# A macaron block with an RWKV mixer: weight sums of the second gate/up phase made in DRAM beforehand, and six seven-product steps a block instead of four

## The chip, the core and the metric

The kernel runs on one core of one Trainium2 chip. The metric is the device time of one execution in microseconds (us), the median of several runs. Before the change it is 1986.32 us (three runs, 1985.78 to 1986.51).

## What is computed

One layer for 256 tokens of width 2048, all in float32: a half-weighted SwiGLU feed-forward (FFN), a mixer (an RWKV-7 scan branch and a pooling branch), and a second FFN.

```python
D_MODEL = 2048; SEQ = 256; D_FF = 5632
def _swiglu(x, w_gate, w_up, w_down):
    return (jax.nn.silu(x @ w_gate) * (x @ w_up)) @ w_down
...
f = _swiglu(_rmsnorm(h, ln_ffn1_pre[l]), ffn1_gate[l], ffn1_up[l], ffn1_down[l])
h = h + MACARON_WEIGHT * _rmsnorm(f, ln_ffn1_post[l])
mx = _hybrid_mixer(_rmsnorm(h, ln_mix_pre[l]), w_in[l], ...)
h = h + _rmsnorm(mx, ln_mix_post[l])
f = _swiglu(_rmsnorm(h, ln_ffn2_pre[l]), ffn2_gate[l], ffn2_up[l], ffn2_down[l])
h = h + MACARON_WEIGHT * _rmsnorm(f, ln_ffn2_post[l])
```

Each gate and up matrix is 2048 x 5632, each down matrix 5632 x 2048. All weights are streamed from DRAM while the products run.

## The kernel before, in words

**Products in three parts.** A float32 operand is split into a high part, rounded by ScalarE (`CAST` to `wH`), and a low part, `wL = w - wH`, by VectorE (`split`). A product is three matmuls (`mm3`): high by high, high by low, low by high. So each weight tile of 128 x 1024 costs ScalarE one cast, VectorE one subtraction, and TensorE twelve matmuls of 512 columns (two row tiles, two halves of the tokens, three parts). The instructions are recorded and emitted later, so every one of them stands at line 525 in the profile, and work is told apart by the names of the tiles.

**The gate/up phase.** The 5632 columns are eleven blocks of 512. A block multiplies the tokens by 512 columns of gate (`f`) and of up (`l`), for two token halves. Its 16 row tiles go in pairs k, k+1. A pair is done either plainly (`Columns.pair`: 24 matmuls for the pair, from two loads of 512 KB) or as a "quad" in Winograd's form of Strassen's method: seven products instead of eight, 21 matmuls. With w(k,l), w(k,f), w(k+1,l), w(k+1,f) for the four weight tiles of 128 x 512 (row tile k or k+1, up or gate), the weight side needs two first sums, kept in `t13`: w(k,l) + w(k,f) and w(k+1,f) + w(k,f); then `t2` = w(k,l) + the second of them; and the last sum `t4` = w(k+1,l) + t2. `Columns.early` loads the tiles, makes the sums and does four of the products; `Columns.late` loads w(k+1,f) and w(k+1,l) once more into `vc` and does the other three, t4 among them. Between them stands `join`, which adds the four part results in PSUM. The table `GATE2` (L50, `GATE1` at L49 for the first FFN) gives the quads of each block: none in the first two, three in the third, then four. `block_seq` (L1016) interleaves a block's own pairs and its late quads with the early quads of the block after it.

Of four quads in a block one (index 3, `GATE_ACC`, L56) has its t13 made by transfers: two loads of w(k,f), then two accumulating transfers issued by GpSimd (`accum_op`). The other three have t13 made by VectorE in one `t<-w,w` instruction of 128 x 1024. The same is done with two of the ten quads in each half of the down phase (`DOWN_ACC`, L55, in `Columns.quad`).

**Who sets the order.** `Plan` simulates the five engines, the transfers and the buffers, and emits each engine's instructions in the order that it finds. TensorE's products stand in the order of the code; VectorE, ScalarE, GpSimd (POOL) and SyncE (SP, which issues nearly all loads) take the ready instruction with the earliest due time. On the chip each engine then executes its list strictly in order, and waits on semaphores where its inputs are not there. Loads go into five buffers `w32` and borrowed "units" (`u`), split weights into five `wH` and `wL`.

**Stages by time in the profile:** first gate/up to about 452 us, first down phase to 687, mixer (input projections `w_in`, two scan chains of small steps, output projections) to about 1340, second gate/up to 1740, second down to the end. In the mixer the chain's small steps run among large products: its `Z` tiles are copied and its powers `g`, `n`, `rs` computed on POOL.

**`KEPT`** (L116): the gate/up results are turned and pass through DRAM (`cx`); of the first `KEPT` tiles of four the split halves are made at once and the raw copy is fetched again for the quads of the down phase, of the later ones the raw copy stays in SBUF and is split when the down phase comes to it. The down phase's quads begin at row tile 4 * `KEPT`. `normed` makes the normalised tokens, and `sums` the token-side sums that the quads need, one call for two quads.

## Time and profile before

| what | value |
|---|---|
| median of three runs | 1986.32 us |
| the profiled execution's own time | 1987.15 us |
| its span, first to last instruction | 1985.4 us |
| TensorE busy | 1974.6 us (99%), 9692 matmuls |
| VectorE busy | 1813.0 us (91%) |
| ScalarE busy | 1210.7 us (61%) |
| GpSimd busy | 118.8 us (6%) |
| moved by the 16 DMA engines | 503.19 MB, 253 GB/s on the mean |
| granted TensorE clock | 0.999 |

The span is 1.75 us shorter than the profiled execution's time, which is 0.83 us above the median. Busy rows of one engine may overlap by the pipeline's depth: where VectorE's instructions follow each other without a gap, the distance between two starts is the price, not the row's length. A row of a chain "x12" is twelve instructions after each other. In rows by windows, (x) is the number of instructions, DMA the busy share of the 16 DMA engines, and GB/s what they moved.

### The profile page before, as it was taken

What the parts mean: (1) busy time and instruction counts of PE and PEld (TensorE: products, weight loads), DVE (VectorE), ACT (ScalarE), POOL (GpSimd) and SP (SyncE); (2) the same over time, 40 slices, a digit from 0 to 9 for tenths busy, and PEclk for the clock granted to TensorE, in tenths of its full rate; (3) what the DMA queues carried; (4) which work ended last, traced back from release to release, by engine and by line L of the source; (5) the groups of instructions that cost most, each with busy time, mean ns of one, the idle gap of its engine ahead of it and who ended that gap; (6) DMA issues with size and microseconds to landing.
All of it is one profiled execution on the core that took longest, in us unless ns stands there. A gap on an engine that the chain in (4) does not pass through costs nothing.

```text
span 1985.4 us, 28410 instructions
## 1 busy us (share of the span) xinstructions
PE 1974.6 (99%) x9692; PEld 1630.8 (82%) x9692; DVE 1813.0 (91%) x2303; ACT 1210.7 (61%) x1552; POOL 118.8 (6%) x190
## 2 busy tenths in 40 slices
...
GB/s 319 323 266 283 276 317 312 278 257 228 242 198 274 261 259 277 216 167 252 178 194 190 128 322 262 240 258 241 273 307 293 317 287 286 255 230 236 204 287 144
DMA packets 278000, 503.19 MB, mean 253 GB/s; under 512 B 25056, under 2 KB 53472, under 8 KB 277856
## 3 DMA queue, kind: packets, MB, share of 16 engines
q1 hardware_dynamic: 267280, 478.96, 73.6%
q0 software_dynamic: 10144, 22.03, 5.3%
...
## 4 chain that ended last, share of the span: by engine, by line
PE 94%; DVE 3%; DMA 1%; ACT 1%; issue 1%; SPq 0%; POOLq 0%; ACTq 0%; DVEq 0%
PE l L525 33%; PE f L525 30%; PE mm L525 22%; PE p L525 6%; DVE wL L525 1%; DMA w<-in_ffn_gate_dram 1%; PE pY L525 0%; PE pA L525 0%; ACT wH L525 0%; PE tr L525 0%; PE pU L525 0%; DMA w<-in_ffn_down_dram 0%; DVE AR L525 0%; DMA w<-in_w_in_dram 0%; PE pSa L525 0%
## 5 line engine op out<-in xcount | busy, mean ns | idle before, releaser
L525 ACT CAST wH<-w 128x1024 fp32r<-128x1024 f32 (+1 forms) x712 | 727.4, 1042 | 508.4 <-PE f L525 105.1
L525 DVE TENSOR_TENSOR wL<-w,wH 128x1024 fp32r<-128x1024 f32 (+1 forms) x712 | 848.8, 1209 | 92.8 <-ACT wH L525 68.8
L525 PE MATMUL l<-wL,xH 128*128 128x512 f32 x828 | 322.3, 389 | 0.0
L525 PE MATMUL l<-wH,xL 128*128 128x512 f32 x828 | 322.2, 389 | 0.0
L525 PE MATMUL l<-wH,xH 128*128 128x512 f32 x828 | 322.1, 389 | 0.0
L525 PE MATMUL f<-wH,xH 128*128 128x512 f32 x608 | 236.6, 389 | 0.0
L525 PE MATMUL f<-wH,xL 128*128 128x512 f32 x608 | 236.6, 389 | 0.0
L525 PE MATMUL f<-wL,xH 128*128 128x512 f32 x608 | 236.5, 389 | 0.0
L525 PE MATMUL mm<-wL,xH 128*128 128x512 f32 (+1 forms) x568 | 220.2, 388 | 1.1 <-DVE wL L525 1.1
L525 PE MATMUL mm<-wH,xH 128*128 128x512 f32 (+1 forms) x568 | 220.8, 389 | 0.5 <-ACT xH L525 0.5
L525 PE MATMUL mm<-wH,xL 128*128 128x512 f32 (+1 forms) x568 | 219.1, 386 | 0.0
L525 ACT CAST wH<-t 128x1024 fp32r<-128x1024 f32 (+1 forms) x158 | 165.3, 1046 | 81.6 <-PE f L525 32.3
L525 DVE TENSOR_TENSOR wL<-t,wH 128x1024 fp32r<-128x1024 f32 (+1 forms) x158 | 191.5, 1212 | 17.0 <-ACT wH L525 7.9
L525 PEld LDWEIGHTS l<-wL,xH 128*128 128x128 f32 x828 | 155.4, 188 | 32.4 <-DVE wL L525 0.2
L525 PEld LDWEIGHTS l<-wH,xH 128*128 128x128 f32 x828 | 155.4, 188 | 32.3
L525 PEld LDWEIGHTS l<-wH,xL 128*128 128x128 f32 x828 | 155.4, 188 | 32.2
L525 DVE TENSOR_TENSOR t<-w,w 128x1024 f32<-128x1024 f32 (+1 forms) x170 | 167.2, 988 | 7.5 <-DMA w<-in_ffn_down_dram 5.6
L525 PEld LDWEIGHTS f<-wL,xH 128*128 128x128 f32 x608 | 114.1, 188 | 23.7
L525 PEld LDWEIGHTS f<-wH,xL 128*128 128x128 f32 x608 | 114.1, 188 | 23.7
L525 PEld LDWEIGHTS f<-wH,xH 128*128 128x128 f32 x608 | 114.1, 188 | 23.6
L525 PEld LDWEIGHTS mm<-wL,xH 128*128 128x128 f32 x568 | 106.8, 188 | 22.7 <-DVE wL L525 2.3
L525 PEld LDWEIGHTS mm<-wH,xH 128*128 128x128 f32 x568 | 106.7, 188 | 22.5 <-ACT xH L525 0.9
...
## 6 DMA issues: line engine op xcount, KB each, us to landing
w<-in_w_in_dram SPq DMA_DIRECT2D x120, 512.0 KB, 4.5
w<-in_ffn_up_dram SPq DMA_DIRECT2D x106, 512.0 KB, 5.1
w<-in_ffn_up_dram SPq DMA_DIRECT2D x210, 256.0 KB, 5.1
w<-in_ffn_gate_dram SPq DMA_DIRECT2D x102, 512.0 KB, 6.0
w<-in_ffn_gate_dram SPq DMA_DIRECT2D x202, 256.0 KB, 5.0
w<-in_ffn_down_dram SPq DMA_DIRECT2D x96, 512.0 KB, 4.8
w<-in_ffn_down_dram SPq DMA_DIRECT2D x152, 256.0 KB, 4.1
cx<-T SPq DMA_DIRECT2D x33, 512.0 KB, 3.8
```

The source lines that it names most:

```text
L525: ins = o.fn(*[real(x) for x in o.a], **{n: real(x) for n, x in o.k.items()})
```

## The change

1. `GATE2` becomes 0, 0, 6, 6, 6, 6, 6, 6, 6, 6, 5: 53 quads in place of 35 in the second gate/up phase. `GATE1` is as before.
2. `prepare` and `feed`: the two first sums of these 53 quads are made in DRAM ahead of time, for two blocks together. A job copies 128 x 1024 of gate from DRAM to a DRAM tile `pre` (issued by SP), and then adds 128 x 1024 of up or gate to it by an accumulating transfer (issued by POOL, which first waits for the copy). There are 58 jobs, 48 of 512 KB and ten of 256 KB (the last block is alone). They are handed to the planner little by little during the first down phase (0.4 for each pair) and the mixer (1.6 for each of its items), and a job's copy waits for the accumulation three jobs before it.
3. `GMODE2`: in the second gate/up phase `early` loads t13 from `pre` by two transfers on SP, which wait until VectorE has made t13's low part three quads before (`FLIGHT`). Quads of even index (mode 5): ScalarE copies t2 to t4, and one accumulating transfer adds w(k+1,l) from DRAM. Quads of odd index (mode 12): ScalarE copies t2 to t4, and in `late` VectorE adds w(k+1,l) from the tile `vc` that is loaded there anyway. In both, w(k,f), w(k+1,f) and the first w(k+1,l) are not loaded any more.
4. `GMODE1` is 8 for all quads of the first FFN: t13 by VectorE in all (none by transfers), t4 as in mode 12. `DOWN_ACC` goes: in the down phases t13 is made by VectorE in all quads (mode 0).
5. `KEPT` goes from 4 to 3. The planner's own numbers for an accumulating transfer change (`ADDING`, `ADD_RATE`), and it hands out jobs only while its list of transfers is short (`IDLE`).

POOL's list in the first scan chain of the mixer, before. `Z` are the chain's copies, `g` the powers of its group norm:

```order
L525 COPY Z_7508<-ev_7490 64x256
L525 COPY Z_7508<-od_7501 64x256
L525 TENSOR_TENSOR g_1795_9106<-g_1794_9093,mhalf 128x4
L525 COPY Z_7508<-ev_7490 64x256
L525 COPY Z_7508<-od_7501 64x256
L525 TENSOR_TENSOR g_1805_9194<-g_1804_9185,mhalf 128x4
L525 TENSOR_TENSOR g_1815_9323<-g_1814_9307,mhalf 128x4
```

The same place after; `pre` are the accumulations of the jobs:

```order
L540 COPY Z_7586<-ev_7571 64x256
L540 COPY Z_7586<-od_7575 64x256
L540 DMA pre_4_1_119<-in_ffn_gate_dram 128x1024
L540 TENSOR_TENSOR g_1795_9191<-g_1794_9176,mhalf 128x4
L540 DMA pre_5_0_120<-in_ffn_up_dram 128x1024
L540 COPY Z_7586<-ev_7571 64x256
L540 COPY Z_7586<-od_7575 64x256
L540 TENSOR_TENSOR g_1805_9286<-g_1804_9271,mhalf 128x4
L540 DMA pre_5_1_121<-in_ffn_gate_dram 128x1024
L540 TENSOR_TENSOR g_1815_9374<-g_1814_9360,mhalf 128x4
```

Three accumulations now stand between the chain's own steps on POOL; the steps' order among themselves is the same.

SP's list at the same place of the mixer, before (`w` are weights on their way to the products, `cx` and `x` the chain's passage through DRAM):

```order
L525 DMA w_1967_8854<-in_w_in_dram 128x2x512
L525 DMA w_1970_8893<-in_w_in_dram 128x2x512
L525 DMA w_1973_8965<-in_w_in_dram 128x2x512
L525 DMA w_2114_9039<-in_w_in_dram 128x2x512
L525 DMA cx_110<-T_1946_9063 128x2x512
```

And after:

```order
L540 DMA w_1967_8960<-in_w_in_dram 128x2x512
L540 DMA w_1970_9013<-in_w_in_dram 128x2x512
L540 DMA pre_4_1_119<-in_ffn_gate_dram 128x1024
L540 DMA pre_5_0_120<-in_ffn_gate_dram 128x1024
L540 DMA pre_5_1_121<-in_ffn_gate_dram 128x1024
L540 DMA w_1973_9098<-in_w_in_dram 128x2x512
L540 DMA w_2114_9141<-in_w_in_dram 128x2x512
L540 DMA cx_168<-T_1946_9169 128x2x512
```

Three copies of 512 KB now stand ahead of the next weights.

VectorE's list in the middle of the second gate/up phase, before: the sum t13 of two tiles (128x1024), t2 (`w<-w,t`), t4, and low parts `wL`:

```order
L525 TENSOR_TENSOR t_3012_14486<-w_3013_14392,w_3014_14400 128x1024
L525 TENSOR_TENSOR w_3013_14392<-w_3013_14392,t_3012_14486 128x512
L525 TENSOR_TENSOR t_2992_14417<-w_3014_14400,w_3013_14392 128x512
L525 TENSOR_TENSOR wL_14503<-t_2989_14390,wH_14444 128x1024
L525 TENSOR_TENSOR wL_14513<-w_3001_14351,wH_14464 128x1024
L525 TENSOR_TENSOR wL_14523<-w_3004_14360,wH_14482 128x1024
```

And after, in the same block:

```order
L540 TENSOR_TENSOR w_2973_14306<-w_2973_14306,t_2974_14382 128x512
L540 TENSOR_TENSOR wL_14520<-t_2875_14015,wH_14490 128x1024
L540 TENSOR_TENSOR w_2982_14330<-w_2982_14330,t_2983_14450 128x512
L540 TENSOR_TENSOR wL_14537<-w_2973_14306,wH_14522 128x1024
L540 TENSOR_TENSOR wL_14546<-t_2974_14382,wH_14529 128x1024
L540 TENSOR_TENSOR wL_14559<-w_2979_14319,wH_14540 128x1024
L540 TENSOR_TENSOR wL_14573<-w_2982_14330,wH_14548 128x1024
L540 TENSOR_TENSOR wL_14584<-t_2983_14450,wH_14556 128x1024
L540 TENSOR_TENSOR t_2899_14217<-t_2899_14217,w_2989_14348 128x512
```

The 128x1024 sum is gone; more low parts stand between the quads' own sums, and the last row is a t4 finished from the late tile (mode 12).

The diff, cut to its core:

```diff
 GATE1 = [0, 0, 3, 4, 4, 4, 4, 4, 4, 4, 4]
-GATE2 = [0, 0, 3, 4, 4, 4, 4, 4, 4, 4, 4]
+GATE2 = [0, 0, 6, 6, 6, 6, 6, 6, 6, 6, 5]
 OUT_QUADS = ((3, 4, 1.0), (3, 1, 1.0))
 DOWN1 = ((10, 1, 2.0), (10, 1, 1.3))
 DOWN2 = ((10, 1, 2.0), (10, 1, 1.3))
 SCRATCH = 1024
-DOWN_ACC = 6, 8
-GATE_ACC = 3,
+PRE = 2
+FLIGHT = 3
+BACK = 3
+OWN = 2
+IDLE = 2200.0
+PRE_DOWN = 0.4
+PRE_MIX = 1.6
+ADD_RATE = 190.0
+GMODE1 = [[8] * 8] * 11
+GMODE2 = [[5, 12, 5, 12, 5, 12]] * 11
+DMODE1 = [0] * 18, [0] * 18
+DMODE2 = DMODE1
...
-ADDING = 3000.0
+ADDING = 800.0
...
-KEPT = 4
+KEPT = 3
...
+            if "accum_op" in k:
+                o.pace = 1000.0
+                o.dur = o.nbytes / ADD_RATE
...
         def can(o):
+            if o.stream == "back" and dma > now + IDLE:
+                return False
...
-    def four(s, k):
-        q = s.b
-        t13 = q.unit((P, 2, 512), F32, "t13")
-        if k not in s.dma:
-            va, vb = q.raw4(k, s.wf, s.cf, s.wl, s.cl)
-            q.nc.vector.tensor_tensor(out=t13, in0=va,
-                                      in1=vb[:, :1].to_broadcast([P, 2, 512]), op=ALU.add)
-            return va, vb, t13
-        get = lambda k, f: (s.wf if f else s.wl)[k * P:k * P + P,
-                                                 (s.cf if f else s.cl):][:, :512]
-        for i in range(2):
-            q.nc.sync.dma_start(out=t13[:, i], in_=get(k, 1))
-        va, vb = [q.raw().rearrange("p (a c) -> p a c", a=2) for _ in range(2)]
-        q.nc.sync.dma_start(out=va[:, 0], in_=get(k, 0))
-        q.nc.sync.dma_start(out=va[:, 1], in_=get(k + 1, 1))
-        q.nc.sync.dma_start(out=vb[:, 1], in_=get(k + 1, 0))
-        for i in range(2):
-            q.nc.gpsimd.dma_start(out=t13[:, i], in_=get(k + i, i), accum_op=ALU.add)
-        return va, vb, t13
+    def at_w(s, k, f):
+        w, c = (s.wf, s.cf) if f else (s.wl, s.cl)
+        return w[k * P:k * P + P, c:c + 512]
+
+    def load(s, out, k, f):
+        s.b.nc.sync.dma_start(out=out, in_=s.at_w(k, f))
+
+    def plus_w(s, out, k, f):
+        s.b.nc.gpsimd.dma_start(out=out, in_=s.at_w(k, f), accum_op=ALU.add)
 
     def early(s, k):
         q = s.b
         V = q.nc.vector
-        va, vb, t13 = s.four(k)
-        V.tensor_tensor(out=va[:, 1], in0=va[:, 0], in1=t13[:, 1], op=ALU.add)
+        add = lambda o, x, y: V.tensor_tensor(out=o, in0=x, in1=y, op=ALU.add)
         i = s.quads.index(k)
+        mode = s.mode(i)
+        va = q.raw(mode & OWN).rearrange("p (a c) -> p a c", a=2)
+        s.load(va[:, 0], k, 0)
+        if mode & 4:
+            t13 = q.unit((P, 2, 512), F32, "t13")
+            with q.set(behind=q.done[-FLIGHT] if len(q.done) >= FLIGHT else None):
+                for j in range(2):
+                    q.nc.sync.dma_start(out=t13[:, j], in_=s.ready(i, j))
+        else:
+            vb = q.raw(mode & OWN).rearrange("p (a c) -> p a c", a=2)
+            s.load(vb[:, 0], k, 1)
+            s.load(va[:, 1], k + 1, 1)
         if i % 2 == 0:
             s.t4[i] = q.unit((P, 2, 512), F32, "t4")
-        V.tensor_tensor(out=s.t4[i - i % 2][:, i % 2], in0=vb[:, 1], in1=va[:, 1],
-                        op=ALU.add)
-        b11, t2 = q.halves(va)
-        t1, t3 = q.halves(t13)
+        t4 = s.t4[i - i % 2][:, i % 2]
+        if mode & 2:
+            s.plus_w(vb[:, 0], k, 0)
+            s.plus_w(va[:, 1], k, 1)
+            t2 = vb[:, 1]
+            add(t2, va[:, 0], va[:, 1])
+        else:
+            if not mode & 4:
+                if not mode & 9:
+                    s.load(vb[:, 1], k + 1, 0)
+                t13 = q.unit((P, 2, 512), F32, "t13")
+                add(t13, va, vb[:, :1].to_broadcast([P, 2, 512]))
+            t2 = va[:, 1]
+            add(t2, va[:, 0], t13[:, 1])
+        if mode & 9:
+            q.nc.scalar.copy(t4, t2)
+            if mode & 1:
+                s.plus_w(t4, k + 1, 0)
+        else:
+            if mode & 2:
+                s.load(t4, k + 1, 0)
+                add(t4, t4, t2)
+            else:
+                add(t4, vb[:, 1], t2)
+        if mode & 2:
+            b11, t3 = q.halves(va)
+            t1, t2 = q.halves(vb)
+        else:
+            b11, t2 = q.halves(va)
+            t1, t3 = q.halves(t13)
+            q.done.append(q.last_low)
...
         b22, b21 = q.halves(vc)
         i = s.quads.index(k)
-        if i % 2 == 0:
-            s.h4 = q.halves(s.t4[i][:, :min(2, len(s.quads) - i)])
         s.mul("f0", s.sm[k // 2][3], b22)
         s.mul("l0", s.rows(k + 1, 0), b21)
-        s.mul("l1", s.rows(k + 1, 1), s.h4[i % 2])
+        t4 = s.t4[i - i % 2][:, i % 2]
+        if s.mode(i) & 8:
+            q.nc.vector.tensor_tensor(out=t4, in0=t4, in1=vc[:, 1], op=ALU.add)
+        if i % 2 or k == s.quads[-1]:
+            i -= i % 2
+            two = s.quads[i:i + 2]
+            for k, w in zip(two, q.halves(s.t4[i][:, :len(two)])):
+                s.mul("l1", s.rows(k + 1, 1), w)
...
+    def prepare(s, wg, wu, quads, modes):
+
+        s.made = {}
+        nc = s.nc
+        nb = len(quads)
+        blocks = [b for b in range(nb) if any(m & 4 for m in modes[b][:quads[b]])]
+        for g in range(0, len(blocks), PRE):
+            bs = blocks[g:g + PRE]
+            c0, w = bs[0] * 512, len(bs) * 512
+            for i in range(max(quads[b] for b in bs)):
+                if not any(modes[b][i] & 4 for b in bs if i < quads[b]):
+                    continue
+                k = 2 * i
+                for j, (m, kk) in enumerate(((wu, k), (wg, k + 1))):
+                    d = s.dram((P, w), f"pre{g}_{i}_{j}")
+                    for n, b in enumerate(bs):
+                        s.made[b, i, j] = d[:, n * 512:n * 512 + 512]
+
+                    def job(d=d, m=m, k=k, kk=kk, c0=c0, w=w):
+                        with s.set(stream="back", behind=s.last[-BACK], lag=0.0):
+                            nc.sync.dma_start(out=d, in_=wg[k * P:k * P + P, c0:c0 + w])
+                            s.last.append(nc.gpsimd.dma_start(
+                                out=d, in_=m[kk * P:kk * P + P, c0:c0 + w], accum_op=ALU.add))
+                    s.jobs.append(job)
+
+    def feed(s, n):
+        s.owed += n
+        while s.owed >= 1 and s.jobs:
+            s.owed -= 1
+            s.jobs.pop(0)()
...
-            jobs[b].dma = [2 * i for i in GATE_ACC if i < quads[b]]
+            jobs[b].mode = lambda i, b=b: modes[b][i]
+            jobs[b].ready = lambda i, j, b=b: s.made[b, i, j]
...
-               downs, 4 * KEPT, DOWN_ACC)
+               downs, 4 * KEPT, downm)
...
+            J.mode = lambda i, c=c: acc[c // 2][i] if acc else 0
...
+                s.feed(PRE_DOWN)
                 J.pair(k, b)
...
+            s.feed(PRE_MIX)
...
+        s.feed(1e9)
...
+        s.prepare(ffn2_gate[0], ffn2_up[0], GATE2, GMODE2)
...
-              GATE1, DOWN1, (load, turn, squares, finish, scaled))
+              GATE1, DOWN1, GMODE1, DMODE1, (load, turn, squares, finish, scaled))
...
-              at_tok(h2), emit, load_to(h2, lambda h: hsp[1, h]), GATE2, DOWN2)
+              at_tok(h2), emit, load_to(h2, lambda h: hsp[1, h]), GATE2, DOWN2, GMODE2, DMODE2)
```

36 lines of the change are left out of this document (28 added, 8 removed).

## The prediction

> **What bounds the kernel now.** I read the page's busy times first, then who TensorE waited for, then the chain that ended last, then busy times by stage.
>
> ```profile
> span 1985.4 us, 28410 instructions
> PE 1974.6 (99%) x9692; PEld 1630.8 (82%) x9692; DVE 1813.0 (91%) x2303; ACT 1210.7 (61%) x1552; POOL 118.8 (6%) x190
> PE mm L525 <- DVE wL L525: 1.9, 4, 0.7
> PE warm L525 <- POOL ident masks.py:199: 1.5, 1, 1.5
> PE 94%; DVE 3%; DMA 1%; ACT 1%; issue 1%; SPq 0%; POOLq 0%; ACTq 0%; DVEq 0%
> ```
>
> TensorE is idle for 10.8 of 1985.4 us, its longest list of waits is 1.9 us, and 94% of the chain is its own work. Where is even that idle time? The first and the last window of the stages:
>
> ```profile
> 0.00:51.00 51.00, 48.44 (x212) 39.47 (x213) 40.01 (x55) 45.08 (x71) 3.48 (x9) 1.00 0.91 321
> 1945.80:1985.40 39.60, 33.29 (x143) 26.25 (x141) 22.40 (x34) 11.06 (x18) 1.10 (x2) 0.96 0.37 124
> ```
>
> 2.6 us at the start and 6.3 us at the end (second number against the first, the window's length); 1.9 us are left for everything between. So the kernel is as long as its list of matmuls, at a price that the chain in order of time gives:
>
> ```profile
> 1460.30 2.72 PE f L525 x12
> 1465.06 11.56 PE l L525 x51
> ```
>
> 11.56 / 51 = 0.2267 us for one 512-column matmul, with the granted clock at 1.00 in the stage rows. The question is what taking matmuls out leaves as the next limit. In four blocks in the middle of the second gate/up phase (columns: PE, PEld, DVE, ACT, POOL, clock, DMA share, GB/s):
>
> ```profile
> 1505.80:1546.60 40.80, 40.80 (x182) 33.78 (x181) 39.05 (x41) 23.67 (x27) 1.70 (x2) 1.00 0.88 282
> 1546.60:1587.40 40.80, 40.80 (x182) 33.78 (x181) 38.03 (x40) 24.38 (x27) 1.73 (x2) 1.00 0.97 317
> 1587.40:1628.20 40.80, 40.80 (x182) 33.78 (x181) 37.40 (x40) 24.80 (x27) 1.73 (x2) 1.00 0.90 285
> 1628.20:1669.00 40.80, 40.80 (x182) 33.78 (x181) 38.87 (x42) 25.22 (x27) 1.76 (x2) 1.00 0.92 296
> ```
>
> A block lasts 40.80 us = 180 matmuls, and VectorE is busy for 37.4 to 39.1 of it: idle 9.85 us in the four, 2.5 a block. It is the next engine in line.
>
> **TensorE: what goes.** 53 quads for 35 is 18 more, three matmuls saved in each: 54 x 0.2267 = 12.24 us. They lie on the path, since TensorE has no idle time there. Nothing else changes TensorE's list. A six-quad block has 174 matmuls and lasts 39.44 us if TensorE alone sets it.
>
> **VectorE in these blocks.** Starts give the prices, as nothing stands between them:
>
> ```profile
> 1466.07 1.22 DVE L525 TENSOR_TENSOR wL<-w,wH 128x1024 fp32r<-128x1024 f32 x1
> 1467.20 1.22 DVE L525 TENSOR_TENSOR t<-w,w 128x1024 f32<-128x1024 f32 x1
> 1468.34 0.69 DVE L525 TENSOR_TENSOR l<-l,s 128x512 f32<-128x512 f32 x1
> 1468.94 0.69 DVE L525 TENSOR_TENSOR f<-f,s 128x512 f32<-128x512 f32 x1
> ```
>
> 1.135 us for 1024 columns, 0.60 for 512. Before, a block has 22 low parts (8 of plain pairs, 3.5 in each quad), 3 sums t13, 4 t2, 4 t4, and 6 other sums of 512 and a transposition of 1024 for joining and evacuating: 26 x 1.135 + 14 x 0.60 = 37.9 us, which the busy times above bear out. After: 4 + 6 x 3.5 = 25 low parts, no t13, 6 t2, 3 t4, the same 6 and 1: 26 x 1.135 + 15 x 0.60 = 38.5 us. So VectorE's list grows by 0.6 us a block while the block shrinks by 1.36: its slack falls from 2.9 to 0.9 us. Most of its 2.5 us idle now is there because it is ahead of TensorE, and such idle time gives way when it falls behind. What does not give way is the time in which it waits for something of its own. The waits of VectorE from 1424 to 1740.5 us:
>
> ```profile
> DVE wL L525 <- issue: 4.5, 4, 2.6
> DVE wL L525 <- PE f L525: 4.4, 7, 1.2
> DVE wL L525 <- ACT wH L525: 4.1, 4, 2.2
> DVE wL L525 <- PE l L525: 2.4, 5, 1.5
> ```
>
> PE rows are waiting for a buffer: VectorE is ahead. ScalarE's 4.1 us over about eight blocks is 0.5 a block, with "issue" 1.1. Set against a slack of 0.9, that is a loss of 0 to 0.2 us a block. Bounds for eight blocks: nothing (all idle time gives way), and, if the 2.5 us of today stay whole, 38.5 + 2.5 - 39.44 = 1.5 each, 12 us. I take 1.5 us, near the lower end, because the waits that are VectorE's own are near the slack.
>
> Edits beside it, with these rows:
>
> ```profile
> L525 ACT CAST wH<-w 128x1024 fp32r<-128x1024 f32 x16 | 16.3, 1054 | 11.2 <-PE f L525 4.2 <-PE l L525 4.0 <-DMA w<-in_ffn_up_dram 3.0
> L525 ACT COPY u<-l 128x512 f32<-128x512 f32 x2 | 1.2, 584 | 0.0
> L525 DVE TENSOR_TENSOR sf<-x 128x256 f32<-128x256 f32 x24 | 9.1, 421 | 0.0
> L525 POOL DMA_DIRECT2D t<-in_ffn_gate_dram x16 | 14.1, 879 | 678.8 <-DMA t<-in_ffn_gate_dram 152.7 <-PE l L525 140.0 <-DMA w<-in_ffn_gate_dram 111.9
> ```
>
> ScalarE gets one 512-column copy for each quad (t2 to t4) and three more casts a block; it is busy for 23.7 to 25.2 of 40.8 us above, and its cast costs 1.05 us, its copy 0.6: 3 x 1.05 + 6 x 0.6 = 6.8 us more, 32 of 39.4. Hidden. The new third call of `sums` adds four 256-column sums and a low part, 4 x 0.42 + 1.14 = 2.8 us of VectorE in block 1, once. The first gate/up phase has one more t13 on VectorE in the eight four-quad blocks: 37.9 + 1.1 = 39.0 of 40.8 us, and it loses the accumulating transfers there. The down phases put two t13 more in each half on VectorE, 4.5 us in a phase:
>
> ```profile
> 452.00:687.00 235.00, 234.47 (x1040) 193.77 (x1039) 218.42 (x250) 143.72 (x169) 12.49 (x37) 1.00 0.75 240
> ```
>
> 218.4 + 4.5 of 235 us leaves 12 us. Hidden behind TensorE's matmuls; without that cover it would be 1.1 us for each. `KEPT` moves one split per FFN from the gate/up phase to the down phase. I cost these at nothing.
>
> **Transfers.** In the second gate/up phase they hardly change: a block of six quads loads 4 x 512 KB for plain pairs, 33 x 256 KB for quads (three of them accumulations), 10.7 MB for 39.44 us, where it loaded 8 x 512 KB and 27 x 256 KB, 11.3 MB, for 40.80. New are the 58 jobs in the first down phase and the mixer. 48 x 0.524 + 10 x 0.262 = 27.8 MB copied and 27.8 MB accumulated, beside what runs there now; and what the 16 engines can move:
>
> ```profile
> 40.00:60.00 20.00, 20.00 (x90) 16.57 (x89) 20.00 (x25) 16.12 (x23) 0.00 (x0) 1.00 1.05 407
> 445.00:1130.00 685.00, 683.04 (x3988) 563.82 (x3987) 617.83 (x973) 421.09 (x617) 70.97 (x124) 1.00 0.71 219
> q1 hardware_dynamic: 267280, 478.96, 73.6%
> q0 software_dynamic: 10144, 22.03, 5.3%
> ```
>
> The loads named on SP beside the jobs stand in the trace of before from about 445 to 1130 us, so that is their stretch: 55.6 MB / 685 us = 81 GB/s on top of 219. If an accumulation costs two loads, because it reads two operands, 41 more: 341 GB/s against 407 that plain loads reach at their best. That fits with a sixth to spare, and so I cost the contention at nothing on the mean. For what it does locally (TensorE loses 685 - 683.04 = 2.0 us in that stretch today, at the turn to the mixer and in the chain), from -1.9 (all idle time between start and end gone) to a copy's own time, 0.524 / 0.407 = 1.3 us, at each of perhaps three places where loads are already late. I take 0.5 us.
>
> **Waits on queues.** A job's copy stands on SP and waits for the accumulation three jobs back; behind it stand the weights of the mixer's products and the chain's `x` and `cx`. The accumulation stands on POOL and waits for its copy; behind it stand `Z`, `g`, `n`, `rs` of the chain, for which VectorE and TensorE wait. Jobs are 685 / 58 = 12 us apart, three jobs 36; and a landing takes
>
> ```profile
> w<-in_w_in_dram SPq DMA_DIRECT2D x120, 512.0 KB, 4.5
> t<-in_ffn_up_dram POOLq DMA_DIRECT2D x16, 256.0 KB, 6.8
> ```
>
> 4.5 us for a load of a copy's size, 6.8 for an accumulation of half a job's. Copy and accumulation together are under 20 us even if the accumulation doubles, so SP should not stand still. The two loads of t13 wait on SP for VectorE's work three quads back, some 20 us: nothing, while VectorE keeps up.
>
> **Sum.** 12.24 - 1.5 - 0.5 = 10.2 us off the span: 1985.4 - 10.2 = 1975.2. The profiled execution is 1987.15 us, 1.75 over its span, and 0.83 above the median of 1986.32; so 1976.1 for the median.
>
> **Rivals.**
> *VectorE becomes the bound of the second gate/up phase.* For: a list of 38.5 in 39.44 us. Against: its idle time today is mostly room. Price 5 to 12 us of the 12.24, with SP's t13 loads held up as well: 1979 to 1986. Decides from 0.9 us of its own waits a block.
>
> *The jobs fill the DMA engines; slower.* Place: 445 to 1130 us. If data passing through DRAM costs once for each reading and writing (copy 2, accumulation 3), the jobs are 139 MB, 203 GB/s: 422 against 407, and the stretch grows by 685 x (422/407 - 1) = 25 us. By the shares of the queues: q1 takes 0.736 x 1985.4 / 478.96 = 3.05 us a MB, q0 0.053 x 1985.4 / 22.03 = 4.78, the jobs 27.8 x 7.83 = 218 us, and 0.29 x 685 = 199 are free: 19 us over. Time 1993 to 1999. For: POOL's transfers do cost more a MB. Against: a share of 1.05 at 407 GB/s shows that rows of packets overlap, so a share is not capacity. It decides where an accumulation costs over 3.6 loads: (407 - 219 - 41) / 41.
>
> The Trainium skill (HBM Reference, Specifications) gives about 358 GB/s for a core as its part of a domain; by it, counting DRAM passes, the stretch would grow by 685 x (422/358 - 1) = 122 us, to about 2096. The trace's 407 GB/s is above that figure, and the page itself says that a core streaming alone passes it; I give it 1 in 100.
>
> *The chain waits on POOL.* POOL in the first chain now:
>
> ```profile
> 943.51 1.30 POOL L525 COPY Z<-od 64x256 f32<-64x256 f32 x1
> 950.02 1.04 POOL L525 TENSOR_TENSOR g<-g,mhalf 128x4 f32<-128x4 f32 x1 [5.22 <-DVE g L525]
> 952.36 1.16 POOL L525 COPY Z<-ev 64x256 f32<-64x256 f32 x1 [1.29 <-PE pS L525]
> ```
>
> Only 1.3 us of idle time stand before a `Z` copy, and an accumulation now goes in there. Its issue alone is about a microsecond (879 ns in the group above); a copy that has not landed costs up to 4.5 us. With about six such places in each of two chains, 12 x 1 to 12 x 4.5 us if TensorE had nothing else to do, though its list there has large products between. I put it at 5 to 17 us: 1979 to 1991.
>
> *It doesn't do what it says.* TensorE's list has 54 rows fewer, so at most a later stall can undo it.
>
> **How the numbers follow.** A measurement of this kernel can tell about 0.2%, 4 us, from no change: faster is below 1982.3, slower above 1990.3. Forecast (1974 to 1979) 0.64; VectorE bound 0.16, two thirds of it faster; DMA engines full 0.11 (with the page's figure), all slower; POOL 0.09, a third each. Faster 0.64 + 0.11 + 0.03 = 0.78; same 0.05 + 0.03 = 0.08; slower 0.11 + 0.03 = 0.14. The range goes from 1986.32 - 12.24 - 1.9 = 1972.2 up to the end of the VectorE rival, 1986.5; it leaves out the full DMA engines and the worst of POOL, some 0.16.
>
> **What would show it.** Right: blocks of 39.4 us in the second gate/up phase with VectorE at 97 to 98%, TensorE's matmuls 54 fewer, its idle time from 445 to 1130 us within 1 us of 2.0, GB/s there about 300. Wrong: TensorE rows waiting for `wL` in the second gate/up phase (VectorE), for `w` in the mixer with DMA shares near 1 (transfers), or for the chain's tiles behind POOL's accumulations. If accumulations of 512 KB take over 30 us to land, SP stands still and the forecast falls.

## The result and the profile after

The changed kernel takes 1999.18 us (median of 4 runs, 1996.29 to 2003.7), the kernel before 1986.24 beside it (1985.78 to 1986.51): 1.0067 of the time before, 95% interval 1.0054 to 1.008. That is 13 us slower, where 10 us faster was forecast. The profiled execution took 2001.72 us, 1.7 over its span. The lines of its page that answer to those of before:

```profile
span 2000.0 us, 28517 instructions
PE 1974.6 (99%) x9638; PEld 1626.0 (81%) x9638; DVE 1835.6 (92%) x2333; ACT 1283.5 (64%) x1668; POOL 149.0 (7%) x227
q1 hardware_dynamic: 265264, 486.82, 72.6%
q0 software_dynamic: 15472, 44.31, 11.6%
PE 78%; DVE 11%; DMA 6%; issue 3%; ACT 2%; POOL 0%; SPq 0%; DVEq 0%; POOLq 0%; ACTq 0%
```

The 54 matmuls are gone (9638 for 9692), yet TensorE is busy for the same 1974.6 us. So what is left runs slower, by 54 x 0.2267 = 12.2 us, and TensorE is idle for 2000.0 - 1974.6 = 25.4 us where it was 10.8. Idle 14.6 more, slower matmuls 12.2 more, matmuls taken out 12.2 less: 14.6 us, which is the difference of the spans. The mean granted clock fell from 0.999 to 0.994, which is some 10 of the 12.2 us (0.005 x 2000); the rest isn't explained.

Where? Follow the same instructions through both traces: start in the trace after minus start in the one before.

| instruction, and its start before (us) | after minus before (us) |
|---|---|
| last but one pair of `fg` of the first down phase (682.9) | +1.2 |
| first `sgb` of the mixer (704.8) | +5.6 |
| `zt` (778.3) | +16.6 |
| `zt`, second half (981.2) | +24.3 |
| first `T` of `sga`, in the mixer's last part (1179.6) | +26.0 |
| first `T` of the second gate/up phase (1342.0) | +26.2 |
| last `T` of the second gate/up phase (1753.6) | +14.3 |
| end (1985.4) | +14.6 |

The second gate/up phase gained 11.9 us, as forecast. The mixer had lost 26 before it began. Two windows of 40 us inside the second gate/up phase (length, then PE, PEld, DVE, ACT, POOL, clock, DMA share, GB/s):

```profile
1480.00:1520.00 40.00, 40.00 (x178) 33.14 (x177) 39.93 (x43) 31.41 (x37) 2.62 (x3) 1.00 0.83 253
1520.00:1560.00 40.00, 40.00 (x179) 33.10 (x178) 39.75 (x43) 31.94 (x39) 2.59 (x3) 1.00 0.95 314
```

TensorE has no idle time, VectorE almost none: its slack was used up and was just enough. Five blocks there, from `T` to `T`, last 1704.2 - 1506.9 = 197.3 us, 39.46 each.

The stretch with the jobs, whole and by stage:

```profile
445.00:1130.00 685.00, 669.44 (x3769) 549.72 (x3769) 610.04 (x949) 411.64 (x600) 101.95 (x162) 0.99 0.95 285
452.00:687.00 235.00, 234.81 (x1034) 193.02 (x1034) 222.13 (x253) 141.96 (x166) 18.33 (x46) 1.00 0.95 298
687.00:900.00 213.00, 201.51 (x1000) 167.58 (x998) 179.73 (x310) 142.77 (x246) 32.98 (x44) 0.96 0.94 278
900.00:1130.00 230.00, 226.11 (x1708) 183.32 (x1708) 201.45 (x380) 121.76 (x185) 50.64 (x74) 0.99 0.96 277
```

Against 0.71 and 219 GB/s before, the DMA share is 0.94 to 0.96 in each stage, and the rate is 285 GB/s, in which an accumulation counts once. The first down phase stands it: TensorE is busy for 234.81 of 235 us, and why that is so was not measured. The mixer does not: 11.5 us idle in 687 to 900, where the kernel before had 0.7:

```profile
687.00:900.00 213.00, 212.28 (x1095) 178.35 (x1094) 194.24 (x344) 149.54 (x255) 19.39 (x30) 1.00 0.76 233
```

Who is waited for in that stage of the changed kernel, and what a load takes to land (KB, median us):

```profile
PE l L540 <- ACT wH L540: 3.0, 1, 3.0
PE mm L540 <- DVE kL L540: 3.0, 1, 3.0
PE mm L540 <- ACT sgb L540: 2.6, 1, 2.6
PE mm L540 <- DVE wL L540: 2.0, 2, 1.2
```

```profile
w<-in_w_in_dram SPq DMA_DIRECT2D x120, 512.0 KB, 5.7
pre<-in_ffn_up_dram POOLq DMA_DIRECT2D x24, 512.0 KB, 8.2
pre<-in_ffn_gate_dram POOLq DMA_DIRECT2D x24, 512.0 KB, 8.0
```

`wH` and `wL` are the split weights, and they come from a `w` that landed late: 5.7 us on the median where it was 4.5, and the chain that ended last holds loads of `w` of 12.50 us (from 715.65) and 9.87 us (from 745.54). `kL`, a low part of weights that are held longer, and `sgb`, an evacuation by ScalarE, are something else, taken up below. The clock falls behind these pauses (PE busy is the second number, the clock the one ahead of the DMA share):

```profile
700.00:710.00 10.00, 7.03 (x26) 5.45 (x25) 9.02 (x23) 7.18 (x22) 2.23 (x1) 0.79 0.93 311
710.00:720.00 10.00, 10.00 (x40) 8.07 (x40) 7.34 (x16) 5.26 (x10) 5.66 (x8) 0.86 0.86 185
760.00:770.00 10.00, 6.33 (x18) 4.43 (x17) 9.19 (x13) 7.90 (x16) 2.29 (x5) 0.70 0.83 249
770.00:780.00 10.00, 10.00 (x44) 8.18 (x44) 7.78 (x10) 6.13 (x8) 4.43 (x10) 0.96 1.02 288
```

After 2.97 us of idle time at 703.6 us TensorE is busy without a break from 710 to 720 and the granted clock is 0.86. In the timeline the fourteen matmuls that follow the pause start some 0.43 us apart instead of 0.2267, about 3 us more: this pause cost its own length and as much again.

### The profile page after: what moved, and what is told of

Its sections match the earlier page's. It is cut to its first block, busy times and chain, and to the rows that moved or that the text cites. A ratio compares the mean times of both kernels' runs of the same rounds, so it can differ in the third digit from the quotient of the medians.

```text
span 2000.0 us, 28517 instructions
## 1 busy us (share of the span) xinstructions
PE 1974.6 (99%) x9638; PEld 1626.0 (81%) x9638; DVE 1835.6 (92%) x2333; ACT 1283.5 (64%) x1668; POOL 149.0 (7%) x227
## 3 DMA queue, kind: packets, MB, share of 16 engines
q0 software_dynamic: 15472, 44.31, 11.6%
## 4 chain that ended last, share of the span: by engine, by line
PE 78%; DVE 11%; DMA 6%; issue 3%; ACT 2%; POOL 0%; SPq 0%; DVEq 0%; POOLq 0%; ACTq 0%
PE l L540 30%; PE f L540 24%; PE mm L540 18%; DVE wL L540 5%; PE p L540 3%; DMA w<-in_ffn_down_dram 3%; DVE t L540 2%; DMA w<-in_w_in_dram 1%; ACT wH L540 1%; DMA cx<-T 1%; DVE xL L540 1%; DMA w<-in_ffn_gate_dram 1%; DVE w L540 0%; PE pA L540 0%; DVE h L540 0%
## 5 line engine op out<-in xcount | busy, mean ns | idle before, releaser
L540 PE MATMUL l<-wH,xL 128*128 128x512 f32 x810 | 315.4, 389 | 0.0
L540 ACT CAST wH<-t 128x1024 fp32r<-128x1024 f32 (+1 forms) x185 | 193.6, 1046 | 115.1 <-DVE t L540 54.0
L540 DVE TENSOR_TENSOR wL<-t,wH 128x1024 fp32r<-128x1024 f32 (+1 forms) x185 | 224.8, 1215 | 5.6 <-ACT wH L540 1.8
L540 PE MATMUL f<-wH,xL 128*128 128x512 f32 x536 | 208.6, 389 | 0.0
L540 PE MATMUL f<-wH,xH 128*128 128x512 f32 x536 | 208.6, 389 | 0.0
L540 PE MATMUL f<-wL,xH 128*128 128x512 f32 x536 | 208.5, 389 | 0.0
L540 PE MATMUL f<-wL,sH 128*128 128x512 f32 x322 | 125.8, 391 | 0.0
L540 PE MATMUL f<-wH,sH 128*128 128x512 f32 x322 | 125.7, 391 | 0.0
L540 PE MATMUL f<-wH,sL 128*128 128x512 f32 x322 | 125.7, 390 | 0.0
L540 PEld LDWEIGHTS mm<-wH,xL 128*128 128x128 f32 x568 | 107.6, 189 | 21.2
```

What stands on the lines that cost most here:

```text
L540: ins = o.fn(*[real(x) for x in o.a], **{n: real(x) for n, x in o.k.items()})
```

## The experiments

Three theories stood at the outset. **A**: the jobs' transfers take the DMA engines' time, and the loads of the mixer land late. **B**: the jobs' waits hold up the lists of SP and GpSimd. **C**: another edit is to blame.

**The parts taken out, planner free.** `e1_no_jobs` has no jobs; the two loads of t13 read weight rows, so that the transfers of the second gate/up phase stay:

```diff
     def feed(s, n):
+        s.jobs = []
...
-                    q.nc.sync.dma_start(out=t13[:, j], in_=s.ready(i, j))
+                    q.nc.sync.dma_start(out=t13[:, j], in_=s.at_w(k + j, 1))
```

> The changed kernel without the 58 jobs: nothing is copied or accumulated to DRAM beforehand, and the second gate/up phase loads t13 from weight rows instead of the made sums (so the first sums are left out of the computation; the number and size of the loads there are the same). Theory A, the jobs' transfers make the mixer's loads land late: the 26 us lost between 690 and 1130 us come back, 1974 us (1972 to 1977), with the mixer's weight loads landing in 4.5 us on the median instead of 5.9. Theory B, the jobs cost by their places in the lists of SP and POOL: the same time, since the places go too. Theory C, the other edits (KEPT 3, first sums by VectorE in the first FFN) disturb the turn to the mixer: 1990 us or more, with the idle time of TensorE near 700 us still there.

Measured 1977.45 us, 0.9959 of before (0.9946 to 0.9972). All edits but the jobs together come to within 3.4 us of 1986.3 - 12.2 = 1974.1. C falls.

`e2_plain_second` drops `accum_op=ALU.add` from a job's second transfer.

> The jobs' second transfer, which POOL issues, is a plain copy in place of an accumulation (so the first sums are left out): the same number of issues, bytes read from the weights and bytes written, the same waits on POOL and SP; what goes is that the engines read the destination and add. Theory A, and the adding is the costly part: the mixer gets most of its time back, 1976 to 1984 us, landings of weights under 5.3 us. Theory A, and the bytes alone do it: 1988 to 1997 us. Theory B, the waits and places in the lists: 1994 to 2000 us, as changed.

1980.82 us, 0.9973 (0.9963 to 0.9983). The planner counts an accumulation at 190 GB/s (`ADD_RATE`) and a plain transfer at 335 (`RATE`), so it wrote another order; this alone doesn't separate the adding from the order. The next group does.

`e3_back_free` lets a copy wait for the accumulation 60 jobs back instead of 3 (`BACK = 60`).

> A job's copy no longer waits for the accumulation three jobs back (BACK 60 in place of 3, so none ever waits); the amount of transfers is unchanged. Theory B, SP stands still at these copies with the mixer's weights behind them: 10 to 25 us faster than the changed kernel, 1975 to 1990 us. Theory A: no gain, 1995 to 2005 us, or worse, if more of them bunch together.

2004.89 us, 1.0093 (1.0072 to 1.0114). Without that wait it is not faster. B's main wait, SP's on the accumulations, is not the cause. GpSimd did stand still behind the copies. Its waits in the changed kernel from 685 to 1130 us, and the longest total of anybody's waits for GpSimd there:

```profile
POOL pre L540 <- DMA pre<-in_ffn_gate_dram: 157.0, 9, 40.2
ACT Z L540 <- POOL Z L540: 1.6, 1, 1.6
```

157 us went by there, and 2.4 us in all of waiting on what stood behind, against 2.2 in the kernel before. The rival in which the chain waits on GpSimd did not come true.

`e4_gate_down` hands the jobs out earlier (`PRE_MIX = 0.0`, and `s.feed(0.25)` in the gate/up phase's blocks). In its trace 40 of the 58 copies start before 690 us, 18 still behind it.

> The same jobs handed out earlier: 0.25 for each item of the first gate/up phase, 0.4 for each pair of the first down phase, none for the mixer; by the order of the lists some 40 of the 58 copies then stand before the mixer's first weights, 17 in its first part. Theory A, and it is the mixer with its late loads that can't bear them while the FFN phases can: three quarters of the loss gone, 1977 to 1986 us, TensorE still without idle time up to 687 us. Theory A, and the engines are simply full: the idle time appears in the first gate/up phase instead, 1990 to 2005 us. Theory B: POOL and SP have little else to do in the FFN phases, so faster too, 1977 to 1986 us; the lists don't tell it from the first.

2017.45 us, 1.0162 (1.0147 to 1.0177). Now TensorE waits in the first gate/up phase and the first down phase, where it had not (two of the pauses stand at 161.0 and 494.5 us, 3.59 and 4.17 long). Its longest waits from 92 to 900 us:

```profile
PE f L541 <- DVE wL L541: 8.3, 3, 4.2
PE mm L541 <- DVE wL L541: 5.4, 1, 5.4
```

The loss goes where the jobs go, which speaks for A and against a peculiarity of the mixer. (From 690 to 900 us, where 15 copies are left and the share is 0.96, TensorE is still idle for 8.3 us.)

**One order, four amounts of transfers.** These kernels keep the changed kernel's order, instruction by instruction, and change only what is emitted for a job: nothing (`f2`), the copy alone (`f3`), copy and a plain second transfer (`f1`), copy and two plain transfers (`j1`). The edit of `f1`:

```diff
             for o in order:
+                if o.stream == "back":
+                    o.k.pop("accum_op", None)
```

and of `j1`, with a second piece of memory for each job that nobody reads:

```diff
             for o in order:
+                if o.stream == "back":
+                    if o.k.pop("accum_op", None) is not None:
+                        o.fn(out=s.alt[o.i], in_=real(o.k["in_"]))
```

> Every list as in the changed kernel, but without the 58 copies and 58 second transfers; t13 is loaded from weight rows (the first sums are left out). Theory A1: the order that was planned around the jobs does no harm itself, 1974 to 1979 us. Rival: the planned order is part of the loss (loads were put late to make room), 1983 us or more.

> The order of the changed kernel, the 58 copies on SP kept and the 58 second transfers on GpSimd left out (the first sums are left out). Both theories: between the kernel without both in this order (1982.8) and the one with both plain (1986.0), so 1984.4 us, if a copy costs what a plain second transfer does. If it is the second transfer's wait on GpSimd that cost the 3.2 us, 1983; if the copies' places on SP, 1986.

> Every list as in the changed kernel, instruction for instruction; only the jobs' second transfers don't add (plain copies, so the first sums are left out). In the run with plain second transfers before, the planner had also moved things. Theory A1, adding holds the engines longer (its 4 KB packets took 314 to 353 ns, plain ones 190): 1978 to 1984 us, three quarters of the loss gone. Theory B, waits and places in the lists: within 3 us of the changed kernel, 1996 to 2002 us.

> The order of the changed kernel; each of the 58 accumulating transfers is replaced by two plain ones of the same rows, the second into memory of its own that nobody reads (the first sums are left out, so the values are not the reference's). Theory A, the DMA engines' time: an accumulation costs what two loads cost, and that time is what the loads of the weights lack. Two plain transfers take the same time from the engines, so the kernel takes 1996 to 2001 us, near the changed kernel's 1999.2. Theory D, the adding itself: an accumulating packet holds up what stands behind it in a way that plain packets do not. Then the third transfer of a job costs only what the other two do, 1.6 us for 58, and the time is 1986.0 + 1.6 to 3, 1987 to 1990 us.

The row from 445 to 1130 us of `f2`, `f3`, `f1` and `j1`, in this order:

```profile
445.00:1130.00 685.00, 679.47 (x3961) 561.64 (x3960) 622.28 (x976) 420.70 (x613) 64.16 (x116) 1.00 0.69 212
```

```profile
445.00:1130.00 685.00, 679.27 (x3966) 560.56 (x3965) 623.61 (x978) 421.76 (x615) 63.24 (x116) 1.00 0.79 251
```

```profile
445.00:1130.00 685.00, 677.07 (x3947) 558.72 (x3946) 619.72 (x972) 417.70 (x609) 91.46 (x170) 1.00 0.88 289
```

```profile
445.00:1130.00 685.00, 668.59 (x3787) 549.78 (x3787) 611.17 (x951) 412.90 (x603) 111.25 (x210) 0.99 0.95 321
```

| a job is | transfers | DMA share | time (us) | ratio to before, interval |
|---|---|---|---|---|
| nothing (`f2`) | 0 | 0.69 | 1982.82 | 0.9982 (0.9973 to 0.9992) |
| copy (`f3`) | 58 | 0.79 | 1981.96 | 0.9980 (0.9971 to 0.9990) |
| copy + plain (`f1`) | 116 | 0.88 | 1986.03 | 0.9998 (0.9989 to 1.0008) |
| copy + two plain (`j1`) | 174 | 0.95 | 1998.61 | 1.0061 (1.0044 to 1.0078) |
| copy + accumulation (the change) | 116 | 0.95 | 1999.18 | 1.0067 (1.0054 to 1.0080) |

Read it downwards. A set of 58 transfers adds 0.10 and 0.09 to the share, and a third would bring it to about 0.97; the row shows 0.95, in a stretch that by then holds fewer of the kernel's matmuls (3787 for 3947). The first set costs nothing, the second 4 us, the third 12.6. And the last two rows agree within their intervals: an accumulation is worth two plain transfers of its size, both in share and in time. The queue of GpSimd says the same: over `f2` it is busy for 161 us more in the changed kernel (11.6% of 2000.0 us against 3.6% of 1982.2), 5.8 us a MB of accumulation, and for 81 us more in `f1`, 2.9 us a MB. Theory A's number for `j1`, 1996 to 2001, holds, and theory D's, 1987 to 1990, does not. The Trainium skill (Collectives: The Full Stack, Stop ④) describes an addition in the DMA path as read, read, write "with the add free in between". These rows show no cost of the adding beyond a second transfer; whether the second read alone makes it up can't be told, as `j1` also writes twice.

That the loss goes with the time of the engines and not with a rate in GB/s shows in the same rows: `j1` moves 321 GB/s at 0.95, the changed kernel 285, and both lose the same. The load's landing rises with the share, 4.6 us in `f3` and 5.8 in `j1` (the rows of `w_in`, first `f3`, then `j1`):

```profile
w<-in_w_in_dram SPq DMA_DIRECT2D x120, 512.0 KB, 4.6
```

```profile
w<-in_w_in_dram SPq DMA_DIRECT2D x120, 512.0 KB, 5.8
```

There is a second cost in the table, between `e1` (1977.45) and `f2` (1982.82): no job runs in either, and 5.4 us lie between. TensorE's longest waits in `f2`:

```profile
PE mm L544 <- ACT sgb L544: 2.6, 1, 2.6
PE mm L544 <- DVE kL L544: 2.1, 1, 2.1
```

The changed kernel has both rows (2.6 and 3.0, above), `e1` has neither. Nor has `e2`, whose planner also had 116 transfers on its queues, but at the price of plain ones. So the order in which `sgb` and `kL` come late was written around the price of the accumulations. `e2` and `f1` hold the same transfers in the two orders, 1980.82 and 1986.03 us, and give the order's cost a second time: 5.2 us. `e2` also shows that a full stage need not lose much. Its row of the mixer's first part has 4.2 us of idle time at a share of 0.97, where `e1` has 2.4 at 0.77:

```profile
690.00:900.00 210.00, 205.76 (x1062) 171.89 (x1061) 187.68 (x328) 142.74 (x240) 34.53 (x47) 1.00 0.97 315
```

**Spreading the jobs.** Accumulations came in bunches. From the changed kernel's GpSimd in order of time:

```profile
707.77 3.51 POOL L540 TENSOR_TENSOR rs<-rt,mhalf 128x1 f32<-128x1 f32 x1 [12.42 <-DVE rt L540]
711.24 0.58 POOL L540 DMA_DIRECT2D hsp<-fg  x1
711.82 0.93 POOL L540 DMA_DIRECT2D pre<-in_ffn_up_dram  x1
712.40 1.19 POOL L540 DMA_DIRECT2D pre<-in_ffn_gate_dram  x1
```

The `rs` ahead waited 12.42 us for VectorE, and two accumulations were issued within a microsecond of each other behind it. Do such bunches cost time? `g1_back1` lets only one job be under way (`BACK = 1`); `g5_one_at_a_time` and `g7_two` also feed them from the first gate/up phase on (0.11 a step there, 0.3 and 0.85 instead of 0.4 and 1.6), with `BACK` 1 and 2.

> BACK 1: a job's copy waits for the job before it, so at most one job is under way, and two accumulations can't be in flight together; the last of the jobs then stand in the second gate/up phase. Theory A2, bursts do the harm (pairs of accumulations issued within a microsecond or two made loads land after 10 to 13 us): 1977 to 1988 us. Theory A1 without bursts, every accumulation costs some 0.4 us wherever it is: 1994 to 2004 us. Theory B, SP stands still before copies: slower than the changed kernel, over 2005 us.

> All 58 jobs with their accumulations (nothing left out), but one at a time (BACK 1) and spread evenly over the first gate/up phase (0.11 for each item), the first down phase (0.3), and the mixer (0.85): by the lists 16 before the down phase, 13 in it, 24 in the mixer, five behind it. Theory A2, bursts do the harm: the mixer loses under 6 us, no idle time in the second gate/up phase, 1975 to 1984 us, faster than before. Theory A1 without bursts, each accumulation costs some 0.4 us wherever it stands: 1993 to 2003 us.

> As the kernel with one job at a time, but two under way (BACK 2), so that pairs can form. Theory A2: between it and the changed kernel, 1980 to 1992 us. Theory A1: 1993 to 2003 us, no different from one at a time.

`g1`: 2050.1 us, 1.0319 (1.0304 to 1.0335). The jobs ran so late (the last accumulation starts at 1761 us) that the last block's sums weren't there, and TensorE stood still in the second gate/up phase, with the clock at 0.71 over these 80 us:

```profile
1690.00:1770.00 80.00, 39.32 (x129) 29.36 (x127) 27.17 (x28) 18.59 (x22) 7.54 (x9) 0.71 0.62 171
```

`g5` and `g7`: 1993.83 us, 1.003 (1.002 to 1.0039), and 1993.61, 1.0034 (1.0021 to 1.0047). Both lie in the range of A1, and it makes no difference whether one or two jobs are under way: these runs do not show that bunches cost anything. The two are some 5 us faster than the changed kernel, and whether the spreading or their other order does it was not separated. 16 us over `e1` remain. `g5` loses nothing in the first gate/up phase at a share of 0.91, and 12.5 us from 445 to 1130 us at 0.87 (0.89, 0.90 and 0.82 by stage):

```profile
51.00:445.00 394.00, 393.86 (x1738) 325.91 (x1737) 378.58 (x398) 256.57 (x297) 13.87 (x19) 1.00 0.91 291
445.00:1130.00 685.00, 672.53 (x3858) 552.32 (x3857) 615.12 (x959) 412.70 (x604) 93.71 (x148) 1.00 0.87 263
```

How much of these 16 us is the new order and how much the transfers wasn't separated. In any case a share below 0.9 does not make a stretch safe.

**The sums made elsewhere.** `e6_sums_on_vector` has six quads with all sums on VectorE (`GMODE2 = [[8] * 6] * 11`), `h1_sums_on_pool` gives t13 to GpSimd (mode 24), with no jobs either.

> Six quads a block without jobs: VectorE makes t13 of every quad (mode 8 in the second FFN too). By the prediction's prices VectorE's list is 38.5 + 6 x 1.135 + 3 x 0.60 = 47.1 us in a block of 39.44 us of matmuls. If VectorE is the next engine in line as the prediction says: 7.7 us a block for eight blocks, 1974 + 61 = 2035 us (2022 to 2045), TensorE waiting for low parts in the second gate/up phase. If VectorE's rows hide something (it has more room than the prices say): under 2010 us.

> Six quads a block and no jobs: t13 of every quad of the second gate/up phase is made by GpSimd in SBUF, which stands idle there (six additions of 128 x 1024 a block). If GpSimd does one in under 5 us and doesn't slow VectorE, the full gain of the 54 matmuls: 1973 to 1979 us. If its additions slow VectorE, whose list has 0.9 us of room a block, by a third while they run: 2 us or more a block, 1988 to 2010 us. If one takes over 6.5 us, GpSimd itself is the bound: over 2000 us.

`e6`: 2034.56 us, 1.0242 (1.0227 to 1.0257). VectorE has no idle time at all in the blocks, TensorE has:

```profile
1450.00:1700.00 250.00, 225.59 (x915) 166.43 (x913) 250.00 (x266) 160.33 (x190) 0.00 (x0) 1.00 0.70 225
```

VectorE is next, as the prediction's working said, and the change's transfers do lift it off the path. `h1`: 2082.49 us, 1.0481 (1.0467 to 1.0494), worse than leaving the sums on VectorE. The page's row of the sums, then VectorE's largest group from 1480 to 1520 us:

```profile
L540 POOL TENSOR_TENSOR t<-w,w 128x1024 f32<-128x1024 f32 x53 | 198.3, 3743 | 287.7 <-DMA w<-in_ffn_gate_dram 99.1
```

```profile
L540 DVE TENSOR_TENSOR wL<-w,wH 128x1024 fp32r<-128x1024 f32 x12 | 18.8, 1585 | 0.0
```

A sum takes 3.74 us on GpSimd on the mean (about 1.2 on VectorE), and VectorE's low part takes 1.59 us on the mean of that window where the changed kernel's takes 1.22. It isn't that all of them are slower: in the timeline most take 1.21, and four beside a sum take 1.92, 2.83, 3.37 and 3.39 us. This is the forecast's case of a slowed VectorE, but the time lies far above its 1988 to 2010 us; what else is in it was not separated.

**The clock by itself.** `p1_pauses` is the kernel before, with six pauses put into TensorE's list in the first gate/up phase (extra copies on ScalarE of one weight tile, 1 to 6 of them, ahead of its split).

> The kernel before with six pauses put into the first gate/up phase, in blocks 4 to 9: ScalarE copies one weight tile onto itself one to six times, and starts only when TensorE has done its last product before it, so TensorE pauses some 2.2, 3.2, 4.1, 5.1, 6.0 and 7.0 us, 28 us together. If a pause costs only itself: 1986 + 28 = 2014 us, and the granted clock stays 1.00. If a pause of about 2.6 us or more also lowers the clock for a while, as the changed kernel's windows read (0.83 in the 20 us around a pause of 2.97 us, 1.00 around one of 1.25): some 3.4 us more for each of five, 2031 us, with a dip behind all but the first.

2004.23 us (two runs), 1.0088 (1.0071 to 1.0105). Most of the short pauses came out much shorter than meant, so neither forecast's sum applies; only the last is long, 6.90 us at 433.8. The row of TensorE on its page, and the windows around the pauses at 390 (1.40 and 0.76 us) and 433.8:

```profile
span 2001.1 us, 28418 instructions
PE 1978.9 (99%) x9692; PEld 1632.8 (82%) x9692; DVE 1814.2 (91%) x2303; ACT 1233.8 (62%) x1573; POOL 119.0 (6%) x190
```

```profile
400.00:410.00 10.00, 10.00 (x46) 8.29 (x45) 9.84 (x10) 5.17 (x5) 0.00 (x0) 1.00 0.82 265
430.00:440.00 10.00, 3.84 (x17) 2.83 (x16) 3.23 (x7) 7.25 (x8) 0.00 (x0) 0.82 0.12 45
440.00:450.00 10.00, 8.79 (x27) 6.73 (x28) 7.69 (x8) 5.81 (x7) 0.00 (x0) 0.66 0.50 156
```

The same 9692 matmuls take 1978.9 - 1974.6 = 4.3 us more, the windows show the lower clock behind the one long pause, and no job is in this kernel. In the last window alone 27 matmuls take 8.79 us, where they would take 6.1 at 0.2267: 2.7 of the 4.3. So a pause is enough for the clock to fall. How long it must be isn't settled by its length alone. The clock also falls in `f2`, around a pause of 2.13 us at 701.1, and in `e1`, behind two of 0.69 and 0.98 us at 751 and 752 (a row of each), while 1.40 and 0.76 us in `p1` left it at 1.00:

```profile
700.00:710.00 10.00, 7.87 (x28) 6.08 (x27) 8.72 (x17) 6.87 (x14) 5.58 (x5) 0.83 0.58 177
755.00:760.00 5.00, 5.00 (x19) 4.03 (x18) 4.73 (x7) 3.92 (x6) 0.00 (x0) 0.77 0.85 288
```

The Trainium skill (TensorE: Matmul & The Clock Gate, Part 1) says that the clock halves after an idle window of about 3.4 us that runs freely. The traces differ in the length: the pauses of `f2` and `e1` are shorter, and the clock fell behind them.

**A version that keeps the sums and beats both?** Five quads a block instead of six. `j3` and `j4` have no jobs and accumulate in SBUF, inside the second gate/up phase; `k1` and `k2` keep the jobs for two or three quads of a block, fed at a third and a half of the rate:

```diff
-GATE2 = [0, 0, 6, 6, 6, 6, 6, 6, 6, 6, 5]
+GATE2 = [0, 0, 5, 5, 5, 5, 5, 5, 5, 5, 5]
...
-GMODE2 = [[5, 12, 5, 12, 5, 12]] * 11
+GMODE2 = [[2, 1, 2, 8, 1]] * 11
```

(`j4` has 2, 1, 2, 1, 1; `k1` 5, 8, 5, 8, 1; `k2` 5, 12, 5, 8, 8.)

> No jobs and no memory scratch: five quads a block, modes 2, 1, 2, 8, 1, so two quads of a block have their first sums made by accumulating transfers straight into the tile in SBUF, three on VectorE, three last sums by accumulation, the rest on VectorE. Nothing is left out. TensorE has 30 matmuls fewer than before, 6.8 us. VectorE's list is 39.6 us in a block of 40.1. If accumulating cost only engine time, six of 256 KB a block beside plain loads fit (about 340 GB/s by two loads each): 1980 to 1983 us. If adding holds up more than its bytes, as the jobs did at 0.23 to 0.28 us each, 54 of them cost 8 or more: 1988 to 1995 us.

> As the one before, modes 2, 1, 2, 1, 1: VectorE's list is 39.1 us in 40.1, seven accumulations a block. If VectorE sets the block in the one before, this one is faster by up to 4 us; if the accumulations do, slower by 1 to 3 us.

> Five quads a block, modes 5, 8, 5, 8, 1, nothing left out: two quads of a block have their first sums from DRAM, so 20 jobs instead of 58, fed at 0.14 and 0.55 instead of 0.4 and 1.6 over the same stretch. TensorE has 30 matmuls fewer than the kernel before: 6.8 us. VectorE's list is 39.0 us in a block of 40.1. Theory A with a threshold (transfers cost nothing while the DMA engines' share from 445 to 1130 us stays below about 0.85): the share there becomes 0.70 + 20/58 x 0.27 = 0.79, like that of the copies alone, so the jobs cost nothing and the time is 1980 to 1982 us, the first version faster than both kernels. Theory A without a threshold (each transfer costs in proportion): 20/58 of the 13 to 17 us, 5 to 6 us, so 1985 to 1987.

> The same with modes 5, 12, 5, 8, 8: three quads of a block from DRAM, 30 jobs, fed at 0.2 and 0.8, nothing left out. VectorE's list is 38.5 us in 40.1; two accumulations a block in the second gate/up phase. The share from 445 to 1130 us becomes 0.70 + 30/58 x 0.27 = 0.84. With a threshold: 1980 to 1983 us; in proportion: 1987 to 1989.

`j3`: 1991.18 us, 1.0025 (1.0014 to 1.0035); `j4`, with one accumulation more in a block, 1995.44, 1.0047 (1.0032 to 1.0062). `j4`, which relieves VectorE, is the slower one, so by the forecast the accumulations set the block and not VectorE. The second gate/up phase of `j3` shows what the mixer did, a share near 1 and idle time:

```profile
1450.00:1750.00 300.00, 295.69 (x1293) 241.98 (x1292) 288.69 (x306) 199.26 (x234) 30.35 (x35) 1.00 0.95 296
```

`k1`: 1983.21 us (12 runs, 1982.19 to 1988.97), 0.9989 (0.998 to 0.9997), between the two forecasts. It is the only version with the whole computation that is faster than before, by 0.1%, less than the 0.2% that the prediction set as what can be told. The profiled execution took 1988.97 us: behind pauses of 1.17 and 0.84 us at 812 us its clock falls too. `k2`: 1991.86 us, 1.0034 (1.0021 to 1.0047). The rows of `k1`, then of `k2`:

```profile
445.00:1130.00 685.00, 680.26 (x3935) 561.07 (x3935) 620.09 (x968) 419.52 (x611) 87.34 (x135) 0.99 0.79 240
687.00:900.00 213.00, 209.72 (x1060) 176.20 (x1059) 187.00 (x321) 146.44 (x245) 33.53 (x37) 0.98 0.86 261
```

```profile
445.00:1130.00 685.00, 677.69 (x3951) 557.97 (x3950) 619.28 (x972) 418.61 (x610) 89.53 (x145) 1.00 0.84 253
687.00:900.00 213.00, 207.06 (x1060) 172.33 (x1059) 186.11 (x323) 144.29 (x250) 29.48 (x41) 0.99 0.92 274
```

Both shares came out as worked out, 0.79 and 0.84, and yet a threshold on the mean of 685 us is wrong: `k2` should then have taken 1980 to 1983. A cost in proportion, 1987 to 1989, is too low as well. In the stage that loses, 687 to 900, its share is 0.92, near the changed kernel's 0.94, since 11 of its 30 accumulations and 10 of its copies are issued there. That the local share decides is argued from these rows only; `e2`, with 0.97 in that part of the mixer and 1980.82 us, speaks against the share alone, and a `k2` with its jobs kept out of that stage wasn't run.

## Why the prediction was wrong, step by step

- **12.24 us from 54 matmuls: right.** The phase gained 11.9 us.
- **VectorE loses 1.5 us there: right in kind, a little too dear.** A block lasts 39.46 us, forecast 39.44 for TensorE alone; VectorE's busy share is 99%, not 97 to 98. Between the two landmarks of the phase only some 0.3 us are missing. The rival in which VectorE becomes the bound did not come true.
- **Edits costed at nothing: nearly right.** `e1` holds them all and is 3.4 us over the ideal 1974.1, the 1.5 for VectorE included.
- **Transfers at 0.5 us: the step that failed.** "That fits with a sixth to spare, and so I cost the contention at nothing on the mean." The size of an accumulation was right, two loads (`j1`), and so was the demand of 341 GB/s counted that way (212 in `f2` and three times 27.8 MB in 685 us make 334). What failed is the capacity it was set against: 407 GB/s, the best 20 us of plain loads in another stage. The row that the prediction shows for the stretch itself, 219 GB/s at a share of 0.71, comes to 219 / 0.71 = 308 GB/s at a share of 1, less than the demand; and `j1`, whose jobs are all plain transfers, moves 321 GB/s at 0.95. The prediction had the better sum in hand, under a rival: jobs 27.8 x 7.83 = 218 us of engine time, 199 free, 0.71 + 218 / 685 = 1.03. It set it aside with "a share is not capacity". As an exact limit it isn't one, and orders differ in what they stand (`e2`, `g5`); but in one order the time grew as the free engine time went. Measured: -0.9 for the copies, +4.1 for their second transfers, +13.2 for adding in them, 16.4 us.
- **Waits on queues at nothing: right, as far as the runs show.** SP's wait costs nothing (`e3`). Copies landed in 6.5 us and accumulations in 8.0 to 8.2, together under the 20 assumed. GpSimd's waits for the copies, 157 us, held up next to nothing. Its bunches behind `rs` were not foreseen; a cost of theirs isn't shown (`g5`, `g7`).
- **Not in the sum: the order that the planner writes around the jobs**, 5.4 us (`e1` to `f2`) or 5.2 (`e2` to `f1`), with the waits for `sgb` and `kL`.
- **Not in the sum: the clock.** In the profiled execution the idle time grew by 14.6 us and the matmuls by 12.2. A wait was priced at its length; here it cost nearly twice that. This is no further term: it is inside the 16.4 and the 5.4 us.

Adding up: 1974.1 + 3.4 + 5.4 - 0.9 + 4.1 + 13.2 = 1999.3, measured 1999.18. These are steps from one measured kernel to the next, so they must add up and prove nothing by it. The rival of full DMA engines, 1993 to 1999, is what happened, its price by queue shares 19 us for a measured 16.4; it had 11 in 100. That its time came so near is in part luck: the order's 5.4 us were in no rival, and its 4.78 us a MB for GpSimd's queue, a mean over plain and accumulating transfers, was too little (5.8 above). Of the signs of being wrong that the prediction named, the trace after shows TensorE waiting for `w` in the mixer with DMA shares near 1, with the wait standing one step later, at `wH` and `wL`.
